# Two-layer decoder trunk on one core: six raw weight blocks and four pairs of rounded blocks and remainders in place of four and five, and a unit's load issued in two parts

## The chip, the core and the metric

The kernel runs on one core of a Trainium2 chip. The metric is the device time of one execution in microseconds; the lower the better. A program on one core shows a single span, and runs of it are compared by their medians.

## The reference

```python
for i in range(2):                       # x: (1, 512, 1024) float32
    if i == 0:
        x = x + dilated_attention_mixer(rmsnorm(x, attn_norm), w_qkv, w_attn_out)
    else:
        x = x + pooling_mixer(rmsnorm(x, pool_norm), w_pool_in, w_pool_group, pool_scale)
    x = x + swiglu_ffn(rmsnorm(x, ffn_norm[i]), w_gate_up[i], w_down[i])
return rmsnorm(x, final_norm)
```

The attention mixer has three groups of eight heads of width 128, with windows of 128, 512 and 2048 positions at strides 1, 4 and 16 and a bias that falls with distance; the outputs of matching heads are merged by their softmax denominators. The pooling mixer takes trailing means over 2, 4, 8 and 16 positions less the token, and a linear map for each of four channel groups. The feed-forward part is `(silu(h @ w_gate) * (h @ w_up)) @ w_down` with an inner width of 2816. All of it is float32.

## The kernel before

**Precision.** TensorE multiplies rounded float32 numbers. So each weight block and each activation is kept as a rounded part and a remainder, and each product is made of three matmuls: rounded by rounded, rounded weight by remainder, remainder of the weight by rounded (lines 412, 413 and 414 in `mult`, 277, 278 and 280 in `Product.add`). `split` makes the two parts: ScalarE copies the block to the rounded type (line 101), VectorE subtracts (line 102).

**Units of weights.** Weights come from memory as units in the order in which TensorE uses them. A `Plain` unit is one block of 128 x 1024 that is split and used by 24 matmuls of width 512. A `Pair` unit holds four quarters of a block product that is done with seven half-size products in place of eight; it needs four split blocks: `b` (blocks), `s` (sums), `m` (more, made of `a` and `b` by two additions on VectorE, lines 178 and 179) and `l` (last, half as wide). Its load fills three raw buffers: `b` by a DMA of SyncE (line 160) onto which a DMA of GpSimd adds another quarter (line 163), `a` (line 161) and `c` (line 162). The split `b` is made of raw `a`, the split `s` of raw `b` with the sum on it, the split `l` of raw `c`. In the names of the trace and of the order a raw buffer is `raw` or `rawhalf`, a split pair is `whi` and `wlo`, or `halfhi` and `halflo`.

**Rings and the pump.** The raw blocks and the split pairs stand in rings (`BUFS`, line 41): five pairs `w`, two half-wide pairs, four raw blocks, two half-wide raw blocks. A buffer is written again once its last reader is `done`. `pump` (line 191) issues, when the program is written, every load that has room, and then one split step if its ring has room; it is called once after each turn of TensorE, so loads and splits are laid between the turns in program order on each engine. All the order is thus set by the sizes of the rings; each engine runs its instructions in that order.

**Turns.** A gate and up unit is worked off by `chain` (line 474) in seven turns of 12 matmuls of width 256 (nine for the down projection's first two groups): `b` by "11", `s` by "1", `m` by "2", `b` by "21" (after which the buffer of `b` is free), `s` by "3", `m` by "22", `l` by "4". Two of the sums are carried over from one PSUM bank to another by a copy on ScalarE (lines 490 and 498), which the next turn of that bank adds to. The copies stand in ScalarE's order between the splits and the activations of the unit before (lines 1097 to 1101). The attention projections use `seven` (line 421) and, for the values, `values12` (line 560).

**The rest that is named later.** `prepare` makes the normed inputs and their sums and differences for the block products (lines 522 to 532); its tiles come out of the raw ring. Line 552 evacuates a projection from PSUM with the row's scale, among them the values `vt` of the first heads, which TensorE then transposes (line 631). `hide` and the `pieces` behind it (lines 997 to 1042) split the hidden activations for the down projection.

Of the kernel before, what the change touches and what calls it, by code (L numbers as in the profile page):

```python
# [11 lines left out]
OP = mybir.AluOpType  # L12
# [3 lines left out]
P = 128  # L16
# [21 lines left out]
NPLAIN = 5  # L38
WARM = 6
NSOLO = 3  # L40
BUFS = {"w": 5, "half": 2, "raw": 4, "rawhalf": 2}
COLS = {"w": D, "half": D // 2, "raw": D, "rawhalf": D // 2}
FIXED = 12
SLOTS = 16
# [7 lines left out]
def trunk(ctx: ExitStack, tc: tile.TileContext, xT, norms, w_first, w_qk, w_qkp, w_v0, w_v0p, w_v12, w_out, w_pair, w_down, w_down0, w_down1, w_down2, w_pin, w_pgrp,  # L52
          consts, ident_in, invcnt_in, outT):
    nc = tc.nc
# [48 lines left out]

    rings = {ring: [] for ring in BUFS}

    class Held:


        def __init__(self, ring):
            self.live = True  # L110
            n = COLS[ring]
            if ring in ("w", "half"):
                self.t = [wpool.tile([P, n], F32R, tag=ring + c, name=ring + c, bufs=BUFS[ring]) for c in ("hi", "lo")]
            else:
                self.t = wpool.tile([P, n], F32, tag=ring, name=ring, bufs=BUFS[ring])
            rings[ring].append(self)
# [4 lines left out]
    def room(ring, n=1):  # L121
        old = rings[ring]
        return all(not t.live for t in (old[len(old) - BUFS[ring] + i] for i in range(n) if len(old) + i >= BUFS[ring]))

    class Plain:
# [7 lines left out]
        def load(self):  # L133
            self.raw = Held("raw")
            o = 0
            for src in self.srcs:
                nc.sync.dma_start(self.raw.t[:, o:o + src.shape[-1]], src)
                o += src.shape[-1]
# [6 lines left out]
    class Pair:  # L145
# [2 lines left out]

        def __init__(self, src):
            self.src, self.q, self.w = src, src.shape[-1] // 4, {}  # L150
            loads.append((self, {"raw": 2, "rawhalf": 1}, self.load))

        def steps(self):
            return [(self, "w", self.blocks), (self, "w", self.sums), (self, "w", self.more), (self, "half", self.last)]

        def load(self):
            q = self.q
            self.a, self.b, self.c = Held("raw"), Held("raw"), Held("rawhalf")
            b = self.b.t[:, :2 * q]
            nc.sync.dma_start(b, self.src[:, :2 * q])  # L160
            nc.sync.dma_start(self.a.t[:, :2 * q], self.src[:, q:3 * q])
            nc.sync.dma_start(self.c.t[:, :q], self.src[:, :q])
            nc.gpsimd.dma_start(b.rearrange("p (a c) -> p a c", a=2),  # L163
                                self.src[:, None, 3 * q:].to_broadcast([P, 2, q]), accum_op=OP.add)

        def made(self, name, ring, v, n):
            self.w[name] = Held(ring)
# [21 lines left out]
    loads, steps, units = deque(), deque(), deque()  # L189
# [129 lines left out]
    def product(layer):  # L319
        return Product(KC, stream(layer)).add(range(KC)).p  # L320
# [221 lines left out]
    with tc.tile_pool(name="opool", bufs=1) as opool:  # L542
        early = opool.tile([P, HEADS, S], F32R, tag="o", name="early")
        with tc.tile_pool(name="apool", bufs=1) as apool:
# [336 lines left out]
            for c in range(2):  # L881
                p = product(0)
# [68 lines left out]
    with tc.tile_pool(name="fpool", bufs=1) as fpool:  # L951
# [232 lines left out]
        for i in (1, 0):  # L1184
            raw = Held("raw")
# [213 lines left out]
```

## Time and profile before

| | us |
|---|---|
| median of three runs | 1248.03 |
| lowest and highest | 1247.94, 1249.01 |
| profiled execution, its own time | 1248.75 |
| its span | 1247.0 |
| TensorE busy in the span | 1233.6 |
| weight loads of TensorE busy | 1169.0 |
| VectorE busy | 1012.9 |
| ScalarE busy | 679.2 |
| GpSimd busy | 155.0 |

The span is that of the instructions in the trace; the profiled execution's own time is 1.75 us longer. In the rows below a line has the start in the span, the duration, the engine (PE for TensorE, DVE for VectorE, ACT for ScalarE, POOL for GpSimd, SPq for the DMA queue of SyncE), the line of the kernel, the operation, and its tiles as out<-in; in square brackets stands how long the engine was idle ahead of it, and what ended that. The granted clock of TensorE is 0.997 of full speed over the span.

### The profile page before, as it was taken

How to read it: one execution, taken by the hardware profiler on the slowest of the kernel's cores; microseconds unless marked ns; L12 is line 12 of the kernel's file. 1: busy time of each engine (PE TensorE's matmuls, PEld its weight loads, DVE VectorE, ACT ScalarE, POOL GpSimd, SP SyncE). 2: the span in 40 equal slices, each digit the busy share in tenths (PEclk: the TensorE clock that was granted, in tenths of full speed). 3: DMA queues.
4: the chain of work that ended last, by engine and by line, in shares of the span. 5: the costliest groups of instructions: out<-in, count | busy, mean ns of one | idle time of the engine just before them, and what ended most of it. 6: DMA issues, size and time to landing. Idle time of an engine off the chain costs nothing. (4 is left out here: it accounts for less than half of the span.)

```text
span 1247.0 us, 23245 instructions
## 1 busy us (share of the span) xinstructions
PE 1233.6 (99%) x9072; PEld 1169.0 (94%) x9072; DVE 1012.9 (81%) x1687; ACT 679.2 (54%) x1171; POOL 155.0 (12%) x147
## 2 busy tenths in 40 slices
PE   9999999999999999999999999999999999999997
PEld 7889999999999988889999999988789999999997
DVE  7987788879778846798778878798989877888876
ACT  6444554445455544466466556564446646656652
POOL 1111111112111000101111111100310111111100
PEclk9999999999999999999999999999999999999998
DMA  8336556656756434437776686553144776678742
GB/s 284 111 86 175 137 150 151 164 131 161 181 135 160 139 134 132 116 84 186 185 187 163 174 201 168 140 198 121 51 119 109 182 190 179 147 194 204 171 123 68
DMA packets 76719, 189.91 MB, mean 152 GB/s; under 512 B 7600, under 2 KB 15936, under 8 KB 76608
## 3 DMA queue, kind: packets, MB, share of 16 engines
q1 hardware_dynamic: 51696, 142.26, 35.8%
q0 software_dynamic: 24336, 45.63, 22.3%
q8 instruction: 71, 1.16, 0.4%
q10 hardware_dynamic: 576, 0.52, 0.1%
q14 instruction: 40, 0.33, 0.1%
HBM read 186.29 MB, written 2.10 MB: 151 GB/s over the span
## 5 line engine op out<-in xcount | busy, mean ns | idle before, releaser
L101 ACT ACTIVATE whi<-raw 128x1024 fp32r<-128x1024 f32 (+2 forms) x315 | 318.6, 1016 | 247.8 <-PE seed L413 74.9
L102 DVE TENSOR_TENSOR wlo<-raw,whi 128x1024 fp32r<-128x1024 f32 (+2 forms) x315 | 366.9, 1168 | 102.9 <-ACT whi L101 101.4
L163 POOL DMA_DIRECT2D raw<-w_pair x34 | 41.1, 1209 | 312.5 <-ACT whi L101 60.0
L412 PE MATMUL sum<-tt,whi 128*128 128x256 f32 x272 | 76.7, 282 | 2.1 <-ACT seed L490 1.2
L413 PE MATMUL sum<-tt,whi 128*128 128x256 f32 x272 | 76.8, 282 | 0.0
L414 PE MATMUL sum<-tt,wlo 128*128 128x256 f32 x272 | 76.2, 280 | 0.0
L101 ACT ACTIVATE halfhi<-rawhalf 128x512 fp32r<-128x512 f32 (+1 forms) x87 | 53.1, 612 | 19.1 <-PE sum L413 12.2
L178 DVE TENSOR_TENSOR raw<-raw 128x512 f32<-128x512 f32 (+1 forms) x87 | 57.5, 661 | 2.3 <-issue 2.2
L179 DVE TENSOR_TENSOR raw<-raw 128x512 f32<-128x512 f32 (+1 forms) x87 | 57.4, 660 | 0.2
L102 DVE TENSOR_TENSOR halflo<-rawhalf,halfhi 128x512 fp32r<-128x512 f32 (+1 forms) x87 | 57.5, 661 | 0.0
L163 POOL DMA_DIRECT2D raw<-w_down x24 | 28.9, 1206 | 213.2 <-DMA raw<-w_down 51.8
L412 PEld LDWEIGHTS sum<-tt,whi 128*128 128x128 f32 x272 | 51.4, 189 | 2.7 <-ACT seed L490 1.4
L498 ACT COPY seed<-sum 128x256 f32<-128x256 f32 x58 | 20.8, 359 | 58.9 <-PE sum L414 58.8
L413 PEld LDWEIGHTS sum<-tt,whi 128*128 128x128 f32 x272 | 51.3, 189 | 0.0
L414 PEld LDWEIGHTS sum<-tt,wlo 128*128 128x128 f32 x272 | 51.1, 188 | 0.0
L412 PE MATMUL sum<-hz,whi 128*128 128x256 f32 x160 | 45.2, 283 | 0.6 <-ACT seed L498 0.3
L413 PE MATMUL seed<-hy,whi 128*128 128x256 f32 x160 | 45.1, 282 | 0.0
L413 PE MATMUL sum<-hz,whi 128*128 128x256 f32 x160 | 45.0, 281 | 0.0
L414 PE MATMUL sum<-hz,wlo 128*128 128x256 f32 x160 | 45.0, 281 | 0.0
L412 PE MATMUL seed<-hy,whi 128*128 128x256 f32 x160 | 44.9, 280 | 0.0
L414 PE MATMUL seed<-hy,wlo 128*128 128x256 f32 x160 | 44.9, 280 | 0.0
L163 POOL DMA_DIRECT2D raw<-w_qkp x18 | 22.0, 1222 | 164.4 <-DMA raw<-w_qkp 89.3
(610 smaller groups left out, 4611.7 us busy)
## 6 DMA issues: line engine op xcount, KB each, us to landing
raw<-w_pair SPq DMA_DIRECT2D x78, 512.0 KB, 4.8
raw<-w_qkp SPq DMA_DIRECT2D x36, 512.0 KB, 4.3
raw<-w_pair POOLq DMA_DIRECT2D x34, 512.0 KB, 7.7
raw<-w_down SPq DMA_DIRECT2D x32, 384.0 KB, 3.8
raw<-w_v SPq DMA_DIRECT2D x18, 512.0 KB, 4.1
raw<-w_qkp POOLq DMA_DIRECT2D x18, 512.0 KB, 7.4
rawhalf<-w_pair SPq DMA_DIRECT2D x34, 256.0 KB, 5.0
raw<-w_down SPq DMA_DIRECT2D x16, 512.0 KB, 4.8
```

Of the source, the lines that this page charges most:

```text
L101: nc.scalar.activation(hi, v, AF.Copy)
L102: nc.vector.tensor_tensor(lo, v, hi.bitcast(F32), op=OP.subtract)
L163: nc.gpsimd.dma_start(b.rearrange("p (a c) -> p a c", a=2), self.src[:, None, 3 * q:].to_broadcast([P, 2, q]), accum_op=OP.add)
L178: nc.vector.tensor_add(a[:, :q], a[:, :q], b[:, :q])
L179: nc.vector.tensor_add(a[:, q:2 * q], a[:, q:2 * q], a[:, :q])
L412: nc.tensor.matmul(dst, w.t[0][:, c], th, start=k == 0 and not onto, stop=False, skip_group_check=onto)
L413: nc.tensor.matmul(dst, w.t[0][:, c], tl, start=False, stop=False, skip_group_check=onto)
L414: nc.tensor.matmul(dst, w.t[1][:, c], th, start=False, stop=k == n - 1, skip_group_check=onto)
L498: nc.scalar.copy(e, c)
```

## The change

The ring of split pairs shrinks from five to four, and that of raw blocks grows from four to six; a split pair of 128 x 1024 takes twice the room of a raw block, so the memory is the same. A `Pair` unit registers two loads in place of one. The first, `load`, needs room for one raw block and issues the sum block `b` with GpSimd's accumulation onto it; the second, `rest`, needs one raw block and one half-wide one and issues `a` and `c`. From line 163 on, a line of the kernel before stands five lines further down in the changed one.

```diff
-BUFS = {"w": 5, "half": 2, "raw": 4, "rawhalf": 2}
+BUFS = {"w": 4, "half": 2, "raw": 6, "rawhalf": 2}
...
-            loads.append((self, {"raw": 2, "rawhalf": 1}, self.load))
+            loads.append((self, {"raw": 1}, self.load))
+            loads.append((self, {"raw": 1, "rawhalf": 1}, self.rest))
...
         def load(self):
             q = self.q
-            self.a, self.b, self.c = Held("raw"), Held("raw"), Held("rawhalf")
+            self.b = Held("raw")
             b = self.b.t[:, :2 * q]
             nc.sync.dma_start(b, self.src[:, :2 * q])
+            nc.gpsimd.dma_start(b.rearrange("p (a c) -> p a c", a=2),
+                                self.src[:, None, 3 * q:].to_broadcast([P, 2, q]), accum_op=OP.add)
+
+        def rest(self):
+            q = self.q
+            self.a, self.c = Held("raw"), Held("rawhalf")
             nc.sync.dma_start(self.a.t[:, :2 * q], self.src[:, q:3 * q])
             nc.sync.dma_start(self.c.t[:, :q], self.src[:, :q])
-            nc.gpsimd.dma_start(b.rearrange("p (a c) -> p a c", a=2),
-                                self.src[:, None, 3 * q:].to_broadcast([P, 2, q]), accum_op=OP.add)
```

The order of the instructions changes with it. The first place is the gate and up unit that TensorE works on around 735 us. On ScalarE before, `raw_8334` and `raw_8335` are the `a` and `b` of one later unit; the split of its sum block is `whi_8486`:

```order
L101 ACTIVATE whi_8420<-raw_8234 128x1024
L1100 ACTIVATE gt_8359<-seed_8364 128x256
L101 ACTIVATE whi_8469<-raw_8334 128x1024
L101 ACTIVATE whi_8486<-raw_8335 128x1024
L1097 ACTIVATE gt_8359<-gt_8359 128x256
L1101 COPY up_8360<-sum_8362 128x256
L101 ACTIVATE halfhi_8578<-rawhalf_8336 128x512
L490 COPY seed_8497<-sum_8495 128x256
L101 ACTIVATE hy_8557<-hid_8490 128x512
L1099 COPY half_8494<-ps_8496 128x256
L101 ACTIVATE hz_8562<-t_8425 128x512
L498 COPY seed_8498<-sum_8495 128x256
```

On ScalarE in the changed kernel, at the same place, the same unit's `a` is `raw_8347`, its `b` is `raw_8251`, and the split of the sum block is `whi_8550`:

```order
L101 ACTIVATE whi_8443<-raw_8247 128x1024
L101 ACTIVATE whi_8485<-raw_8347 128x1024
L1102 ACTIVATE gt_8358<-gt_8358 128x256
L1106 COPY up_8359<-sum_8361 128x256
L101 ACTIVATE halfhi_8599<-rawhalf_8348 128x512
L495 COPY seed_8496<-sum_8494 128x256
L101 ACTIVATE hy_8554<-hid_8489 128x512
L1104 COPY half_8493<-ps_8495 128x256
L101 ACTIVATE hz_8559<-t_8422 128x512
L101 ACTIVATE hu_8582<-t_8422 128x256
L503 COPY seed_8497<-sum_8494 128x256
L101 ACTIVATE whi_8550<-raw_8251 128x1024
```

The split of the sum block has moved from ahead of both copies (lines 490 and 498, now 495 and 503) to behind them.

The second place is between the first two heads. On VectorE before, the two evacuations of values, `vt_474` and `vt_475`, stand close together:

```order
L552 TENSOR_TENSOR vt_474<-seed_476,row_355 128x4x32x4
L663 TENSOR_REDUCE st_522<-s0_524 128x3
L665 TENSOR_REDUCE st_522<-s0_524 128x1
L552 TENSOR_TENSOR vt_475<-seed_562,row_355 128x4x32x4
L666 TENSOR_SCALAR nm_523<-st_522 128x4
L102 TENSOR_TENSOR wlo_588<-raw_501,whi_587 128x1024
L683 SCALAR_TENSOR_TENSOR s12_613<-sum_614,b12_519 128x512
```

On VectorE in the changed kernel, from the second reduction behind `vt_474` up to `vt_475`:

```order
L670 TENSOR_REDUCE st_511<-s0_513 128x1
L527 SCALAR_TENSOR_TENSOR raw_530<-x_78,nrm_84,row_359 128x512
L671 TENSOR_SCALAR nm_512<-st_511 128x4
L527 SCALAR_TENSOR_TENSOR raw_530<-x_82,nrm_84,row_359 128x512
L102 TENSOR_TENSOR wlo_594<-raw_353,whi_593 128x1024
L531 TENSOR_TENSOR raw_531<-raw_530 128x2x256
L102 TENSOR_TENSOR h_537<-raw_530,h_537 128x512
L532 TENSOR_TENSOR raw_531<-raw_531,raw_530 128x256
L102 TENSOR_TENSOR h_540<-raw_530,h_540 128x512
L537 TENSOR_TENSOR raw_531<-raw_531,raw_530 128x256
L102 TENSOR_TENSOR tx_544<-raw_531,tx_543 128x512
L557 TENSOR_TENSOR vt_475<-seed_551,row_359 128x4x32x4
```

A whole preparation of inputs and one subtraction of a split stand between them now. On TensorE before, the transposes of both follow each other, ahead of the next product:

```order
L681 MATMUL ps_620<-qk21_470,qk20_468 128x128
L631 MATMUL seed_633<-ident_85,vt_474 128x128 x4
L631 MATMUL ps_639<-ident_85,vt_475 128x128 x4
L277 MATMUL seed_645<-early_108,whi_385 128x512
L278 MATMUL seed_645<-early_108,whi_385 128x512
```

On TensorE in the changed kernel, the second four stand behind that whole product (24 matmuls into `seed_651`) and one matmul of the next:

```order
L283 MATMUL seed_651<-early_114,whi_389 128x512
L285 MATMUL seed_651<-early_113,wlo_390 128x512
L282 MATMUL sum_682<-early_108,whi_445 128x512
L636 MATMUL ps_645<-ident_85,vt_475 128x128 x4
L283 MATMUL sum_682<-early_108,whi_445 128x512
```

The transposes of `vt_474` stay ahead of the product.

## The prediction

> **What bounds the kernel now.** I read the page first, then the waits of TensorE, then the windows around the only long gaps, then the timeline of each engine inside them.
>
> ```profile
> span 1247.0 us, 23245 instructions
> PE 1233.6 (99%) x9072; PEld 1169.0 (94%) x9072; DVE 1012.9 (81%) x1687; ACT 679.2 (54%) x1171; POOL 155.0 (12%) x147
> 150.00:200.00 50.00, 50.00 (x423) 49.84 (x422) 43.33 (x69) 26.01 (x48) 6.39 (x7) 1.00 0.58 139
> 720.00:725.00 5.00, 4.98 (x42) 4.85 (x41) 4.44 (x8) 2.22 (x4) 1.21 (x1) 1.00 0.72 253
> 730.00:735.00 5.00, 3.79 (x32) 3.58 (x31) 2.05 (x4) 2.43 (x5) 1.20 (x1) 1.00 0.86 209
> 735.00:740.00 5.00, 4.21 (x34) 4.00 (x35) 4.61 (x10) 3.09 (x7) 0.00 (x0) 1.00 0.79 192
> ```
>
> The first two rows say that TensorE is busy for 1233.6 of 1247.0 us, so whatever the change does to loads and splits, at most 13.4 us of idle time can come back, and part of that is the start and the end of the program, which the change doesn't touch. In the windows (length, then busy time and count of PE, PEld, DVE, ACT, POOL, then clock, DMA share, GB/s) the row 150 to 200 is the steady state: 50.00 of 50.00 busy, 423 matmuls, one each 50/423 = 0.118 us, at full clock. The rows 730 to 735 and 735 to 740 are the exception: 32 and 34 matmuls where 42 fit, and PE idle for 1.21 + 0.79 = 2.0 us.
>
> ```profile
> PE sum L412 <- ACT seed L490: 1.4, 2, 1.2
> PE sum L412 <- ACT seed L498: 1.1, 2, 0.8
> PE ps L371 <- POOL rcol L363: 1.1, 1, 1.1
> 733.33 0.28 PE L414 MATMUL ps<-tt,wlo 128*128 128x256 f32 x1
> 734.82 0.39 PE L412 MATMUL sum<-tt,whi 128*128 128x256 f32 x1 [1.21 <-ACT seed L490]
> 737.65 0.28 PE L414 MATMUL seed<-tb,wlo 128*128 128x256 f32 x1
> 738.73 0.39 PE L412 MATMUL sum<-tt,whi 128*128 128x256 f32 x1 [0.79 <-ACT seed L498]
> ```
>
> By starts, the first gap costs 734.82 - 733.33 - 0.12 = 1.37 us and the second 738.73 - 737.65 - 0.12 = 0.96 us: 2.33 us, in one unit of the gate and up product. In both, TensorE waits for a copy from PSUM to PSUM on ScalarE (lines 490, 498) that reads what it has itself just finished. Why that copy is late stands in ScalarE's timeline, and what held ScalarE in those of SyncE, GpSimd and VectorE:
>
> ```profile
> 732.34 1.06 ACT L101 ACTIVATE whi<-raw 128x1024 fp32r<-128x1024 f32 x1 [3.49 <-PE sum L414]
> 733.31 0.40 ACT L1097 ACTIVATE gt<-gt 128x256 f32<-128x256 f32 x1
> 733.86 0.63 ACT L101 ACTIVATE halfhi<-rawhalf 128x512 fp32r<-128x512 f32 x1
> 734.39 0.37 ACT L490 COPY seed<-sum 128x256 f32<-128x256 f32 x1
> 715.82 0.33 SPq L160 DMA_DIRECT2D raw<-w_pair  x1
> 723.46 1.21 POOL L163 DMA_DIRECT2D raw<-w_pair  x1 [8.00 <-ACT seed L490]
> 733.43 1.23 DVE L102 TENSOR_TENSOR wlo<-raw,whi 128x1024 fp32r<-128x1024 f32 x1 [2.95 <-ACT whi L101]
> 737.32 0.42 DVE L1035 TENSOR_TENSOR t<-hid 128x256 f32<-128x256 f32 x1
> 737.77 0.63 ACT L101 ACTIVATE hz<-t 128x512 fp32r<-128x512 f32 x1 [1.59 <-DVE t L1035]
> raw<-w_pair SPq DMA_DIRECT2D x78, 512.0 KB, 4.8
> raw<-w_pair POOLq DMA_DIRECT2D x34, 512.0 KB, 7.7
> ```
>
> ScalarE stood idle for 3.49 us before the split of the unit's sum block (732.34), and the copy of line 490 is queued behind that split and three short operations. The page names PE as the releaser. I read it as the load: the block was asked for at 715.82, its accumulating part was issued at 723.46, and 723.46 + 7.7 (the last row) = 731.2, one microsecond before the split starts. VectorE was idle for 2.95 us for the same split; its subtraction at 733.43 and the operations behind it then arrive late at line 1035 (737.32), for which ScalarE's hz waits 1.59 us (737.77), and the copy of line 498, behind hz, makes the second gap. So both gaps have one cause.
>
> **The change part by part.** *Issue in two parts, six raw blocks.* A unit's sum block now takes its raw buffer alone; in the ring of six instead of four the slot that it takes was last used by the sum block three units earlier, not two. A unit is 84 matmuls by 0.118 = 9.9 us, so that load is asked for about 9.9 us sooner. What it needs is 4.8 + 7.7 = 12.5 us from issue to landed sum; here it had 732.34 - 715.82 = 16.5 us and still came last, because the accumulation was issued only at 723.46, 7.6 us after the first part. With 16.5 + 9.9 = 26.4 us the load is not last. The same split now also stands behind both copies in ScalarE's order, and the copies no longer have to pass it. I take back both gaps: -2.33 us. Bounds: nothing below 0 if another operation of that unit holds ScalarE, -2.33 at most.
>
> Two gaps of the same kind are shorter, and may go too or grow:
>
> ```profile
> 814.02 0.40 PE L277 MATMUL ps<-a,whi 128*128 128x512 f32 x1
> 814.65 0.39 PE L412 MATMUL sum<-hz,whi 128*128 128x256 f32 x1 [0.23 <-ACT seed L490]
> 826.59 0.39 PE L278 MATMUL ps<-a,whi 128*128 128x512 f32 x1
> 827.32 0.39 PE L412 MATMUL sum<-hz,whi 128*128 128x256 f32 x1 [0.35 <-ACT seed L498]
> ```
>
> A 512 wide matmul of these takes 0.21 us from start to start, so they cost 0.42 and 0.52 us. No load shows behind them; I leave them in, with bounds of -0.94 and +0.94.
>
> The Trainium skill ("DMA: Bandwidth & Descriptors", section "Anatomy of one DMA — SWDGE (gpsimd) path") fits a DMA of GpSimd as 2.0 us plus bytes / 436e3, an estimate of 3.2 us for 512 KB. By that rule the sum would have landed by 723.46 + 3.2 = 726.7, the load would not be what held the split, and the sum would stand as in the second rival below. The trace has 7.7 us for the median of 34, and the measurement decides.
>
> *Four pairs of rounded blocks.* A split can now start only when the block four before it has been multiplied, not five, so it is made a turn or more later. The unit with least time is a down projection block (384 KB), where a turn is nine matmuls:
>
> ```profile
> 1095.92 0.27 PE L414 MATMUL seed<-hy,wlo 128*128 128x256 f32 x1
> 1096.12 0.85 ACT L101 ACTIVATE whi<-raw 128x768 fp32r<-128x768 f32 x1 [0.53 <-PE seed L413]
> 1097.00 0.96 DVE L102 TENSOR_TENSOR wlo<-raw,whi 128x768 fp32r<-128x768 f32 x1 [0.34 <-ACT whi L101]
> 1097.87 0.41 DVE L1117 TENSOR_TENSOR x<-x,sum 128x256 f32<-128x256 f32 x1
> 1100.46 0.28 PE L412 MATMUL ps<-hx,whi 128*128 128x256 f32 x1
> ```
>
> With four buffers the s block of the next unit goes into the buffer whose last reader starts at 1095.92, and its own first reader starts at 1100.46: 4.5 us. The rows 1096.12 and 1097.00 show what a split needs after such a release: it ends at 1097.96, 2.0 us after 1095.92. The margin is 2.5 us. A gate and up unit has four turns of 12 in that stretch instead of four of 9, 12 x 0.118 = 1.4 us more, and needs 0.5 us more for its wider split (the rows 732.34 and 733.43). I cost this at nothing, covered by that margin; when ScalarE or VectorE has more than 2.5 us of other work queued ahead, each such unit pays the rest. Behind the waiting split on ScalarE stand, in the unit around 735, the gate's activation (line 1105 of the changed kernel) and the split of the next block, for which nothing of TensorE waits within the turn; the subtraction on VectorE holds back the residual additions, which TensorE needs only when their bank comes round.
>
> *Order in the first heads.* Six raw blocks let the projections' loads and the values' preparation run further ahead, and in VectorE's order this preparation now stands between the two evacuations of line 552 that feed the transposes of line 631:
>
> ```profile
> 54.40 0.93 DVE L663 TENSOR_REDUCE st<-s 128x3 f32<-128x768 f32 x1
> 55.44 1.07 DVE L552 TENSOR_TENSOR vt<-seed,row 128x512 f32<-128x512 f32 x1
> 58.14 1.41 DVE L522 SCALAR_TENSOR_TENSOR raw<-x,nrm,row 128x512 f32<-128x512 f32 x2
> 47.59 0.69 DVE L526 TENSOR_TENSOR raw<-raw 128x512 f32<-128x512 f32 x1
> 60.06 1.29 DVE L102 TENSOR_TENSOR h<-raw,h 128x512 fp32r<-128x512 f32 x2
> 48.79 0.43 DVE L527 TENSOR_TENSOR raw<-raw 128x256 f32<-128x256 f32 x1
> 55.87 0.60 PE L631 MATMUL seed<-ident,vt 128*128 128x128 f32 x4
> ```
>
> Between them now stand the two products of line 522 (1.41), one subtraction of 1.23 (as at 733.43), line 526 (0.69), two h (1.29), lines 527 and 532 (0.43 each) and one tx (as one h, 0.64): 6.1 us by durations. Neighbours overlap a little (55.44 + 1.07 = 56.51, and in the row above 54.40 + 0.93 = 55.33, with a reduction between them), so I take 5.8. The second evacuation then ends near 56.5 + 5.8 = 62.3. TensorE's second four transposes have moved too, behind a product of 24 matmuls by 0.21 = 5.1 us and one more: they come up near 55.87 + 0.6 + 5.3 = 61.8. So TensorE waits 0.5 us and some latency, and I take +0.6; 0 to 5.8 are the bounds (all cover kept, all lost), 0.6 lies next to the lower since the cover is 5.3 long and is in the order.
>
> *Other moves.* GpSimd's accumulations come a unit earlier, before some scalar work of the heads; its 155.0 us of 1247.0 leave room, so this costs nothing. The line 363 operation behind the 1.1 us wait of the final norm stays where it was. The bytes moved are the same.
>
> *Sum.* The profiled execution took 1248.75, span 1247.0; the median of the three runs is 1248.03, 0.72 less. 1248.75 - 2.33 + 0.6 = 1247.02, and less 0.72 this gives 1246.3.
>
> **The rivals.** *Everything near goes.* The 0.94 us of the two short gaps also vanish, since they too wait for copies behind ScalarE, and the first head pays nothing: 1248.03 - 2.33 - 0.94 = 1244.8, or 1244.3 with half of the 1.07 us by which the three runs of before differ (1247.94 to 1249.01). For it: the copies stand ahead of late splits now. Against: their gaps show no idle load.
>
> *The ring holds the split.* The profile names PE as the releaser of the split at 732.34, not a DMA. If so the lead of the load is worth nothing and one rounded buffer fewer makes the split a turn later, 12 x 0.118 = 1.42 us; the copies may still be ahead of it, but VectorE is as late as before for line 1035 and the second gap stays: 1246.3 + 1.42 = 1247.7. Against: the timing of 723.46 + 7.7.
>
> *Slower: late splits in the down projection.* There are 24 such units, three groups of four in each layer. If their splits have more than 2.5 us of other work ahead of them, they decide: one ScalarE split (0.85) and one VectorE split (0.96) with three residual additions (0.41 each) ahead make 3.0, and each unit pays 0.5 us: 24 x 0.5 = 12, in half of them 6. That gives 1246.3 + 6 = 1252.3. For it: VectorE is at 81%, and in windows at 4.61 of 5.00. Against: in the row of 1097.00 it had idled 0.34 us before the split, so it was not backed up there.
>
> **How the numbers follow.** A measurement of this kernel can tell about 0.2% from no change, 2.5 us: faster is under 1245.5, slower over 1250.5. My forecast, 1246.3 (from 1245.7 without the 0.6 up to 1251.5), has 0.53, of which 0.02 lies over 1250.5 (the first head pays nearly all of its 5.8: 1246.3 - 0.6 + 5.8 = 1251.5); everything near goes 0.22, all of it faster; the ring holds the split 0.09, within; late splits 0.16, slower. So faster 0.22, same 0.51 + 0.09 = 0.60, slower 0.02 + 0.16 = 0.18. The range from 1244.3 to 1250.2 leaves out the late splits (0.16) and the upper end of the first case (0.03).
>
> **What would show it.** Right: PE full (42 matmuls) in the windows around 730 to 740, no wait for line 490 or 498 over 0.4 us, the split of the sum block behind both copies and without idle time ahead of it; a wait of TensorE below 1 us at the transposes near 62 us. Wrong: waits of PE for wlo of line 102, which the trace of before does not have at all, repeated once a unit; or the same gap on another copy.

## The result, and the profile after

The two kernels ran beside each other 22 times each: 1248.99 us before, 1247.47 us after, ratio 0.9988 with a 95% interval of 0.9983 to 0.9994. That is 1.5 us less (0.7 to 2.1). The forecast was 1.7 less, 1246.3 against a median of 1248.03. The measured time lies 1.2 us over the forecast and inside its range (1244.3 to 1250.2); the later runs put the median of before 1 us higher. By the prediction's own limits, faster under 1245.5 and slower over 1250.5, this is no change; that the difference can be told from zero is owed to the 22 runs of each kernel.

A second thing shows in these runs: before, they lie between 1246.62 and 1250.86, 4.24 us apart; after, between 1246.80 and 1248.18, 1.38 apart.

The profiled execution of the changed kernel, from its page:

```profile
span 1246.1 us, 23146 instructions
PE 1234.5 (99%) x9072; PEld 1170.0 (94%) x9072; DVE 1014.3 (81%) x1687; ACT 679.5 (55%) x1171; POOL 157.2 (13%) x147
raw<-w_pair POOLq DMA_DIRECT2D x34, 512.0 KB, 6.9
```

The span is 0.9 us shorter; the idle time of TensorE was 13.4 us before and is 11.6 now. Here are entries of its list of waits (two of 0.2 us are left out), then the windows at the two places of the prediction:

```profile
PE seed L838 <- DVE idle L835: 1.2, 1, 1.2
PE ps L376 <- POOL rcol L368: 1.1, 1, 1.1
PE ps L636 <- DVE vt L557: 0.6, 1, 0.6
PE sum L417 <- ACT seed L503: 0.4, 1, 0.4
PE sum L417 <- DVE x L1122: 0.2, 1, 0.2
```

```profile
60.00:65.00 5.00, 4.39 (x22) 3.40 (x21) 5.00 (x10) 3.36 (x6) 0.00 (x0) 1.00 0.99 188
730.00:735.00 5.00, 5.00 (x43) 4.96 (x43) 4.99 (x9) 3.84 (x7) 0.72 (x1) 1.00 0.66 136
735.00:740.00 5.00, 5.00 (x44) 5.00 (x43) 4.19 (x8) 3.40 (x7) 1.20 (x1) 1.00 0.76 201
```

TensorE is full where it had 32 and 34 matmuls, and the two waits of over 0.8 us for the copies are gone. A new wait of 0.61 us stands at the transposes. The timeline of the unit around 735 shows why the gaps are gone, in the order of time: SyncE's issue of the sum block, GpSimd's accumulation, the addition on VectorE that reads the sum (now line 183), and ScalarE with both copies (now lines 495 and 503) and the split:

```profile
712.98 0.33 SPq L161 DMA_DIRECT2D raw<-w_pair  x1
719.53 1.20 POOL L162 DMA_DIRECT2D raw<-w_pair  x1 [7.53 <-DVE x L1119]
733.95 0.69 DVE L183 TENSOR_TENSOR raw<-raw 128x512 f32<-128x512 f32 x1
734.04 0.36 ACT L495 COPY seed<-sum 128x256 f32<-128x256 f32 x1 [0.50 <-PE sum L419]
737.30 0.37 ACT L503 COPY seed<-sum 128x256 f32<-128x256 f32 x1
738.20 1.06 ACT L101 ACTIVATE whi<-raw 128x1024 fp32r<-128x1024 f32 x1 [0.53 <-PE seed L418]
```

This accumulation landed 6.7 us after its issue, at 719.53 + 6.7 = 726.2. The first to read the sum is no longer the split but the addition at 733.95, 7.7 us later, and the copy of line 495 waits for nothing but TensorE's own turn. In the trace of before, the accumulation issued at 723.46 took 8.7 us: it landed at 732.2, and the split started at 732.34. So the load did hold that split, as the prediction read it, although the profile names PE.

How the lead came about isn't quite what was forecast. From the issue of the load to the first reader are 733.95 - 712.98 = 21.0 us now, against 16.5 before. The forecast of 26.4 was made for the split, which starts 738.20 - 712.98 = 25.2 us after the issue; that these two numbers are close is luck. The load was to be asked for 9.9 us sooner. It is issued 715.82 - 712.98 = 2.8 us sooner, or 4.5 us when one counts that TensorE runs 1.6 us later at this place; the rest of the 25.2 comes from a split that is 5.9 us later. Just ahead of the issue VectorE ends the subtraction of an earlier split (712.00 + 0.96 = 712.96), which I read as what made the buffer free.

Where the time went is best read from a row that both traces have, the first transpose of each norm's factors (line 371, now 376). Starts in us, before and after:

| place | before | after | gained or lost since the row above |
|---|---|---|---|
| first norm | 31.70 | 32.00 | -0.30 |
| behind the attention | 506.48 | 507.79 | -1.01 |
| behind the first feed-forward part and pooling | 908.95 | 908.17 | +2.09 |
| last norm | 1238.95 | 1238.06 | +0.11 |

The same row ahead of the pooling, at 850.45 before and 849.74 now, puts 2.0 of the 2.1 us in the first feed-forward part. So in these two executions that part gained 2 us, the attention gave 1.0 back, and 0.3 went at the program's start, where the order is that of before. When the starts of all matmuls are compared one by one, some 0.7 us of the attention's loss stands at the first head, and 0.13 us each at 157, 265 and 373 us, where the products of queries and keys stand in another order on TensorE.

### The profile page after: what moved, and what is told of

It reads as the page before. It is cut to its first block, busy times and chain, and to the rows that moved or that the text cites. A ratio compares the mean times of both kernels' runs of the same rounds, so it can differ in the third digit from the quotient of the medians.

```text
span 1246.1 us, 23146 instructions
## 1 busy us (share of the span) xinstructions
PE 1234.5 (99%) x9072; PEld 1170.0 (94%) x9072; DVE 1014.3 (81%) x1687; ACT 679.5 (55%) x1171; POOL 157.2 (13%) x147
## 4 chain that ended last, share of the span: by engine, by line
PE 90%; issue 4%; DVE 4%; DMA 1%; POOL 1%; ACT 0%; DVEq 0%; POOLq 0%
PE sum L417 9%; PE sum L418 9%; PE sum L419 9%; PE seed L417 6%; PE seed L418 6%; PE seed L419 6%; PE ps L418 4%; PE ps L417 4%; PE ps L419 4%; PE ps L283 3%; PE ps L285 3%; PE seed L283 3%; PE seed L285 3%; PE seed L282 3%; PE ps L282 3%
```

## The experiments

Two theories stood against each other. "Load": the time before is lost because the sum block lands late, and the change asks for it a unit earlier. "Order": the time is lost because a split stands ahead of the copies, and four split pairs in place of five move it behind them. Times below are medians, each kernel beside runs of before on the same chip.

**Four pairs, nothing else (e1).**

```diff
-BUFS = {"w": 5, "half": 2, "raw": 4, "rawhalf": 2}
+BUFS = {"w": 4, "half": 2, "raw": 4, "rawhalf": 2}
```

> The kernel before with four split pairs in place of five, raw ring of four and load in one part as before. Its sum-block split stands behind both copies, as in the changed kernel, and the transposes of the second values stand 5 matmuls behind the first, next to the evacuation. Theory 'load' (the gain comes from loads asked for a unit earlier): the sum still lands late, the two gaps at 730 to 740 us stay or move to another instruction, time within 0.5 us of before. Theory 'order' (the gain comes from the split standing behind the copies): both gaps are gone, no wait at the transposes, 2 us below before, 0.9983.

Measured: 1250.61 us, ratio 1.0013 (1.0003 to 1.0023), eleven runs from 1248.79 to 1254.83. "Order" falls: the split stands where it stands in the changed kernel, and the time is worse. "Load" had the mechanism but expected a time within 0.5 us of before. The traced run is the fastest of the eleven, so its trace shows where time goes but not how much the median loses. The two gaps around 735 are gone in it, and the same lateness shows at another reader. From GpSimd, VectorE and TensorE:

```profile
709.19 1.20 POOL L163 DMA_DIRECT2D raw<-w_pair  x1 [7.12 <-DVE x L1111]
716.83 0.69 DVE L178 TENSOR_TENSOR raw<-raw 128x512 f32<-128x512 f32 x1 [1.68 <-issue]
721.44 0.41 DVE L1117 TENSOR_TENSOR x<-x,sum 128x256 f32<-128x256 f32 x1
721.91 0.39 PE L412 MATMUL sum<-hu,halfhi 128*128 128x256 f32 x1 [1.21 <-DVE x L1117]
```

The accumulation was issued at 709.19 and landed 7.6 us later, at 716.8; the addition of line 178, which reads the sum, starts at 716.83 after 1.68 us of idle time that the profile puts down to nothing. Everything behind it on VectorE is late, up to the residual addition for which TensorE waits 1.21 us. The load of this unit was issued at 704.53, 12.3 us before the addition; the loads of the next two units have 13.2 and 12.5 us. The prediction's 4.8 + 7.7 = 12.5 leaves no room there. In the changed kernel the accumulation for this addition was issued at 702.06, and VectorE came to it at 715.87 without idle time.

**The load in two parts, nothing else (e2).**

```diff
-BUFS = {"w": 4, "half": 2, "raw": 6, "rawhalf": 2}
+BUFS = {"w": 5, "half": 2, "raw": 4, "rawhalf": 2}
```

(against the changed kernel)

> The load in two parts alone: five split pairs and four raw blocks as before. Both theories: nothing to be seen, 0.9996 to 1.0004, since the raw slot that the sum block waits for and the place of its split (ahead of the copies) are those of before; gaps of 2 us in all stay around 735 us. If the issue in two parts were itself worth something, the sum would land earlier and the time fall by 1 to 2 us.

Measured: 1248.89 us, ratio 1.0001 (0.9991 to 1.0010). The time is as expected. The gaps are not around 735 us, where they were expected, but elsewhere, though the order in that unit is that of before:

```profile
PE sum L417 <- ACT seed L495: 2.0, 3, 1.1
PE sum L417 <- ACT seed L503: 1.1, 2, 0.8
721.66 1.06 ACT L101 ACTIVATE whi<-raw 128x1024 fp32r<-128x1024 f32 x1 [3.12 <-DMA raw<-w_pair]
723.14 0.37 ACT L495 COPY seed<-sum 128x256 f32<-128x256 f32 x1
723.56 0.39 PE L417 MATMUL sum<-tt,whi 128*128 128x256 f32 x1 [1.09 <-ACT seed L495]
```

Here the profile itself names the DMA as what released the split, and the copy and TensorE follow, one unit earlier in the program than in the trace of before. Two more such gaps stand at 1133 and 1137 us, in the second layer, where the trace of before lost 0.23 us by starts. So which unit is hit differs between these two traces, whose kernels have the same rings; one trace of before shows only a sample.

**Six raw blocks and four pairs, load in one part (e3).**

```diff
-BUFS = {"w": 5, "half": 2, "raw": 4, "rawhalf": 2}
+BUFS = {"w": 4, "half": 2, "raw": 6, "rawhalf": 2}
```

> The changed kernel with the load in one part, as before: four split pairs, six raw blocks. Both theories: as the changed kernel, 0.9988 of before, with its wait of 0.6 us at the transposes, since the vt order is the same. If the issue in two parts carries the gain, 0.9995 to 1.0 and gaps at 735 us.

Measured: 1247.49 us, ratio 0.9986 (0.9977 to 0.9995), the wait at the transposes 0.63 us. This is the changed kernel in all that can be told; issuing in two parts adds nothing to the time. The sum block of the unit around 735 is issued at 713.03 here, and at 712.98 in the changed kernel: the lead is that of the six blocks.

**Before, without the accumulations (e5).** The two lines of GpSimd's DMA are taken out.

```diff
-            nc.gpsimd.dma_start(b.rearrange("p (a c) -> p a c", a=2),
-                                self.src[:, None, 3 * q:].to_broadcast([P, 2, q]), accum_op=OP.add)
```

> The kernel before without GpSimd's accumulations: the sum block then holds one quarter alone, so this leaves a part of the block product out. Every order on TensorE, ScalarE and VectorE is that of before; the split of the sum block still stands ahead of both copies. Theory 'load': the sum block has landed about 7.7 us sooner, the two gaps are gone wherever they fell, 2 us below before (0.998), and runs differ by no more than those of the changed kernel (1.4 us). Theory 'order': the gaps stay, 1.000.

Measured: 1245.48 us, ratio 0.9977 (0.9967 to 0.9986), runs from 1244.67 to 1246.76. The split stands ahead of the copies as before, five pairs and four blocks as before, and the gaps are gone:

```profile
720.00:740.00 20.00, 20.00 (x170) 19.96 (x169) 16.56 (x26) 12.58 (x22) 0.00 (x0) 1.00 0.44 141
PE sum L410 <- ACT seed L496: 0.3, 1, 0.3
PE sum L410 <- ACT seed L488: 0.2, 1, 0.2
```

That is 2.9 us (1.7 to 4.1) below before, the most that late sums can cost there. The edit also takes nearly a quarter of the DMA traffic away, 146 MB in place of 190, so transfers land sooner in general (the blocks of the page's w_pair row in 3.6 us in place of 4.8). This run can't part the two; the next one takes the same traffic from the changed kernel.

**After, without the accumulations (e9).** The same edit on the changed kernel.

> The changed kernel without GpSimd's accumulations (a quarter of each block product's sum is left out). Theory 'load': with six raw blocks no step waits for a sum any more, so taking the accumulations away changes nothing: within 0.5 us of the changed kernel, 0.9984 to 0.9992 of before. Rival: sums still land late in some units of some runs; then 1 to 2 us below the changed kernel, as the same edit of before fell by 2.9.

Measured: 1247.07 us, ratio 0.9983 (0.9975 to 0.9992), runs from 1246.36 to 1247.67. It lies 0.4 us below the changed kernel, inside both intervals: with six blocks no wait for sums can be told any more, and less traffic by itself is worth little there. That speaks for the late sums as the main part of the 2.9 us above.

**Every accumulation twice, before (e6) and after (e7).**

```diff
-            nc.gpsimd.dma_start(b.rearrange("p (a c) -> p a c", a=2),
-                                self.src[:, None, 3 * q:].to_broadcast([P, 2, q]), accum_op=OP.add)
+            for _ in range(2):
+                nc.gpsimd.dma_start(b.rearrange("p (a c) -> p a c", a=2),
+                                    self.src[:, None, 3 * q:].to_broadcast([P, 2, q]), accum_op=OP.add)
```

> The kernel before with each accumulation issued twice, so that one quarter is added twice, and the sum block lands some 7 us later. Theory 'load': with two sum blocks in the ring a slot turns over in about 4.8 + 2 x 7.7 + 3 = 23 us for two units, 11.7 us a unit against the 9.9 of TensorE; 84 such units at 1.8 give some 150 us, 60 to 170 over before. Theory 'order': a split waits a little longer behind nothing, some 10 us over before.

> The changed kernel with each accumulation issued twice (one quarter is added twice). Theory 'load': three sum blocks turn over in 23 us for three units, 7.8 us a unit, less than TensorE's 9.9: within 5 us of the changed kernel, far below the same edit of before. Theory 'order': as much over the changed kernel as the same edit is over before.

Measured: before 1441.48 us, ratio 1.1525 (1.1488 to 1.1563), 193 us more; after 1347.94 us, ratio 1.0779 (1.0741 to 1.0817), 100 us more than the changed kernel. The first is a little over the range given. The second was a miss: I had expected 5 us at most. In the first, TensorE waits 34 times for the very copy of the 735 us gap (line 490, here 491):

```profile
PE sum L413 <- ACT seed L491: 81.9, 34, 6.4
```

For the second, GpSimd's timeline in the feed-forward part tells what the turnover of the ring left out:

```profile
raw<-w_pair POOLq DMA_DIRECT2D x68, 512.0 KB, 9.2
627.91 2.47 POOL L163 DMA_DIRECT2D raw<-w_pair  x2 [10.91 <-DMA raw<-w_pair]
640.01 2.44 POOL L163 DMA_DIRECT2D raw<-w_pair  x2 [9.63 <-DMA raw<-w_pair]
653.48 2.44 POOL L163 DMA_DIRECT2D raw<-w_pair  x2 [11.03 <-DMA raw<-w_pair]
```

The second accumulation of a unit waits for the first to land, and GpSimd, which issues in order, waits with it: 9.6 to 11.0 us idle and 2.4 us of issue. It serves a unit in 12.1 to 13.5 us in these rows, while TensorE needs 9.9; a deeper ring can't mend a rate. The Trainium skill says the same of the wait ("DMA: Bandwidth & Descriptors", section "Anatomy of one DMA — SWDGE (gpsimd) path"): a DMA engine waits on no semaphore, the issuing sequencer does. Still, the loss with six blocks is half of that with four. Not all of either loss is waiting: the granted clock fell too (last section).

**Five raw blocks (e10).**

```diff
-BUFS = {"w": 4, "half": 2, "raw": 6, "rawhalf": 2}
+BUFS = {"w": 4, "half": 2, "raw": 5, "rawhalf": 2}
```

> The changed kernel with five raw blocks in place of six: a sum block waits for a slot that comes free about half a unit, 5 us, later than with six and 5 us sooner than with four. Theory 'load': the lead decides, so the time lies between that of four pairs with four blocks (1.0013 of before) and the changed kernel (0.9988), nearer to the latter, 0.9988 to 0.9995, and its runs scatter less than those with four blocks (6.0 us from lowest to highest). If a sixth block is needed at every unit: 1.000 or more.

Measured: 1247.79 us, ratio 0.9991 (0.9982 to 1.0000), runs from 1247.49 to 1248.54, 1.05 us apart. As "load" expected for the time and the scatter, though the interval just reaches 1: a sixth block can't be told from the fifth. The leads say why. In the unit around 735, from the issue of the load to the first reader are 12.5 us with four blocks (four pairs), 19.7 with five and 21.0 with six. The fifth block gives most of the lead, not half of it as I had expected.

**Three pairs (e8).**

```diff
-BUFS = {"w": 4, "half": 2, "raw": 6, "rawhalf": 2}
+BUFS = {"w": 3, "half": 2, "raw": 6, "rawhalf": 2}
```

> The changed kernel with three split pairs in place of four. It prices the margin of 2.5 us that I gave to four: with three a split has a turn less, 1.06 us in the down projection, 1.42 elsewhere, which leaves 1.4 us, and less for the block that two additions precede (0.55 each): close to nothing. If the margin is right: TensorE waits for remainders (line 102) or additions there, 0 to 20 us slower than the changed kernel. If four already stood at the edge: some 0.5 us or more in each of 84 units, 40 us or more.

Measured: 1272.59 us, ratio 1.0193 (1.0179 to 1.0207), 25 us over the changed kernel, between the two cases. The list of waits shows almost nothing of it. The count of matmuls in a steady window does, first with four pairs, then with three:

```profile
650.00:700.00 50.00, 50.00 (x421) 49.89 (x420) 41.47 (x71) 32.60 (x60) 6.00 (x5) 1.00 0.65 158
```

```profile
650.00:700.00 50.00, 49.87 (x410) 48.95 (x409) 41.57 (x69) 32.27 (x61) 6.11 (x6) 1.00 0.67 155
```

Busy time is 49.87 of 50, but 11 matmuls of 421 are missing: 1.3 us lost in five units, in many steps of 0.1 to 0.3 us. One of these steps, from VectorE, ScalarE and TensorE, is the start of an `m` block:

```profile
657.19 0.69 DVE L184 TENSOR_TENSOR raw<-raw 128x512 f32<-128x512 f32 x1
657.97 1.06 ACT L101 ACTIVATE whi<-raw 128x1024 fp32r<-128x1024 f32 x1 [0.40 <-DVE raw L184]
659.06 1.23 DVE L102 TENSOR_TENSOR wlo<-raw,whi 128x1024 fp32r<-128x1024 f32 x1
659.08 0.39 PE L417 MATMUL sum<-tt,whi 128*128 128x256 f32 x1
660.37 0.36 PE L419 MATMUL sum<-tt,wlo 128*128 128x256 f32 x1
```

The split waits for the second addition (ends 657.88) and ends at 659.03; TensorE starts the block at 659.08, 0.3 us late. The remainder ends at 660.29, and TensorE first uses it at 660.37, behind matmuls of another product. So here the additions, the split and the remainder of `m` come last, one behind the other. Four pairs are one step from an edge.

**Moving the preparations (e4 and e11).** Two attempts to get the wait at the transposes back, both on the changed kernel:

```diff
                 scaled_by(VT[c], p, True)
-                prepare(2 + c)
+            for c in range(2):
+                prepare(2 + c)
             scores12(0)
```

> The changed kernel with both evacuations of the first values written ahead of the two preparations that follow. The second evacuation stands next to the first again on VectorE, and its transposes 5 matmuls behind. The wait of 0.6 us at the transposes is gone; 0.6 us below the changed kernel, 2.1 below before, 0.9983.

> The changed kernel with the two preparations written behind the scores of the first head's far groups, so that the second evacuation of values and the far sums both stand ahead of them on VectorE. A subtraction of 1.2 us still stands ahead of the second evacuation. The wait of 0.45 us for the far sums that appeared when the preparations stood between is gone, the one at the transposes (0.5 to 0.6) stays: 0.2 to 0.6 us below the changed kernel, 0.9984 to 0.9988 of before.

Measured: 1247.56 us, ratio 0.9988 (0.9979 to 0.9996), and with the preparations behind `scores12(0)` 1247.67 us, ratio 0.9989 (0.9980 to 0.9998). Neither gained, though both were expected to. From the first of them, VectorE and TensorE:

```profile
55.88 1.21 DVE L102 TENSOR_TENSOR wlo<-raw,whi 128x1024 fp32r<-128x1024 f32 x1
57.08 1.07 DVE L557 TENSOR_TENSOR vt<-seed,row 128x512 f32<-128x512 f32 x1
58.21 0.66 PE L636 MATMUL ps<-ident,vt 128*128 128x128 f32 x4 [0.53 <-DVE vt L557]
74.98 0.63 PE L718 MATMUL ps<-far,const 128*128 128x32 f32 x4 [0.45 <-DVE far L705]
```

The preparations are out of the way, but with them the cover went too: the transposes now stand behind 6 matmuls, not 25, a subtraction of 1.21 us is ahead of the evacuation, and TensorE waits 0.53 us, hardly less than in the changed kernel (0.61). What was moved back holds up the far sums, 0.45 us. In the second the transposes wait 0.54 us and the far sums 0.26.

## Why the prediction was right, point by point

- **Both gaps go: right, and the cause is shown.** Without the accumulations, in the order of before, they vanish (e5); with the load in two parts the profile names the DMA (e2); twice the accumulation makes the copy of line 490 wait in 34 places (e6); and in the trace of before the accumulation landed at 732.2, just ahead of the split at 732.34. The term was sized from one trace, -2.33 us; late sums cost up to 2.9 (1.7 to 4.1) over runs.
- **How much sooner the load comes: mis-sized.** The prediction counted on 9.9 us. Against TensorE it is 4.5, and the lead to the first reader grows from 16.5 to 21.0 us. That is enough, so the gaps went all the same.
- **By which part of the change: half right.** I put the lead down to the issue in two parts and the six blocks together, and named the split's new place behind the copies as a second reason. The runs give it to the raw blocks alone: two parts alone 1.0001, six blocks without them 0.9986. The place behind the copies clears the gaps around 735 in the trace but gains nothing by itself (1.0013): the lateness then goes to the addition of line 178. Six blocks with five pairs, which need more memory, were not run.
- **The transposes: the wait is right, by two errors that cancel.** Forecast +0.6, a wait of 0.61 us, 0.79 us by starts. The second evacuation ends at 62.95 and not at 62.3; TensorE comes up at 62.2 and not at 61.8, since matmuls of width 512 start every 0.23 us here (56.75 to 56.98), where the prediction took 0.21. Nor do the six blocks alone bring the wait: with four pairs and four blocks (e1) a subtraction stands between the two evacuations, and TensorE waits 0.52 us.
- **Two short gaps stay: right in the sum, not in the place.** With 0.21 us from start to start they cost 0.42 and 0.52 us before, and about 0.02 less each with 0.23. Both are gone in the changed kernel, and two others came nearby: 0.53 us at 815.23, for the copy of line 503, and 0.3 at 828.72.
- **Four pairs cost nothing, margin 2.5 us: a little too small, and the margin doesn't hold.** The changed kernel waits 0.25 us near 721 us behind a late split. It also loses 0.13 us at each of 157, 265 and 373 us and 0.3 between 558 and 569; the same losses stand in e1, so they come with the four pairs. Three, with one turn less (1.06 to 1.42 us), should by that margin have had about 1 us to spare and lost 25 in all. What I counted was a split on engines that stand idle when the buffer comes free; the additions before the `m` block and the queue of other work were left out. In the unit shown above it is these additions, the split and the remainder that end last; how the 25 us divide over all units I didn't count.
- **The sum: near, in part by luck.** Over runs late sums may cost more than the 2.33 us of one trace (up to 2.9), and in the traces the new order costs more than the 0.6 forecast (1.0 in the attention alone). Two such errors have opposite signs.
- **The rivals.** "The ring holds the split" is refuted by e5, where the ring is that of before. "Late splits" didn't come at four pairs beyond the 0.25 us above, and came at three. "Everything near goes" didn't come. The Trainium skill ("DMA: Bandwidth & Descriptors", section "Anatomy of one DMA — SWDGE (gpsimd) path") gives by its fit an estimate of 3.2 us for a DMA of GpSimd of this size, which would have freed the load; the accumulating ones here took longer, with medians of 6.9 to 9.2 us in these runs.

No version that computes all of it beats the changed kernel by more than can be told.

## What to carry to other kernels

A transfer in two dependent steps needs the lead of both, and of the wait between; count it from the first issue to the first reader, whichever engine that is, since moving the reader only moves the stall. When a kernel's runs scatter by more than a rival's, a load that lands about when it is needed is one thing to look for: here its traces showed other victims, and the deeper ring took away much of the scatter together with part of the median. And a busy engine can hide small waits: count instructions in a window, not busy time.

## What was not expected of the hardware

Runs lie 4.24 us apart before (22 runs) and 6.04 with four pairs and four blocks (11 runs), but 1.05 to 1.59 in five of the six sets of four pairs with five or six blocks and 2.10 in the sixth (e3). It is less sharp than that in the rest: the sets of before beside the experiments lie 2.38 to 4.35 apart, e2 with the rings of before 2.58, and e5 without the accumulations 2.09. So scatter goes with the lead of one load here, but why the amount differs so from set to set isn't shown. One run of before beside e1 to e4 took 4300.61 us and isn't counted in these; its cause is open.

GpSimd's accumulating DMA of 512 KB had a median of 6.9 to 8.7 us from issue to landing in the runs with one for each unit, and of 8.4 and 9.2 us in the two with twice as many. In those two the granted clock also fell: over the span it was 0.954 in the kernel with the order of before, in the row of the page's slices

```profile
PEclk9999998999999999999999899999999998998998
```

against 0.997 before, and 0.966 against 0.999 in the changed kernel. With the order of before, TensorE was busy 1294.4 us for the same 9072 matmuls, against 1233.6 with one accumulation each, so an estimated 60 of the 193 us are slower matmuls and not waits. With three pairs, where time was lost in small steps, the clock stayed at 0.998.
